# Two extra tokens as zero columns in a Strassen product: 512 columns in one bank for three products of seven

## The chip, the core and the metric

The kernel runs on one core of a Trainium2 chip. The core has five engines that run side by side and meet through semaphores: TensorE (PE, matrix products into PSUM), VectorE (DVE), ScalarE (ACT), GpSimd (POOL) and SyncE (SP, which here only issues transfers). PSUM has eight banks of 512 float32 values per partition; one matmul writes one bank.

The metric is the device time of one execution in microseconds (us), lower is better; the median of the runs is compared.

## The reference

One layer of a decoder trunk on 1,024 tokens of width 1,024, with 16 learned meta tokens ahead of them:

```python
u = rmsnorm(h, mix_norm_pre[l])
proj = u @ w_in[l]
q, f_logit, i_in, g_out, v_pool, gate_a, gate_b = jnp.split(proj, cuts, axis=-1)
a = hgrn2(q, f_logit, i_in, g_out, lbs[l], hgrn_out_norm[l])
p = multiscale_pool(v_pool, pool_proj[l], pool_scale[l])
z = (jax.nn.sigmoid(gate_a) * (a @ w_branch_hgrn[l])
     + jax.nn.sigmoid(gate_b) * (p @ w_branch_pool[l]))
h = h + rmsnorm(z @ w_out[l], mix_norm_post[l])
u = rmsnorm(h, ffn_norm_pre[l])
gt = causal_dwconv(u @ ffn_w_gate[l], ffn_conv_w[l], ffn_conv_b[l])
y = (jax.nn.gelu(gt, approximate=True) * (u @ ffn_w_up[l])) @ ffn_w_down[l]
h = h + rmsnorm(y, ffn_norm_post[l])
return h[:, N_META:]
```

`gate_a` and `gate_b` are 1,024 wide each, the MLP's gate and up 2,816. The convolution `causal_dwconv` looks at a token and the two before it. Because of it the MLP's gate needs two tokens ahead of the 1,024 that are returned: 1,026 in all (`TQ`), which the kernel also uses for the mixer's gates.

## The kernel before

Float32 accuracy comes from splitting every operand into a high and a low part in the fast float32 format (`hi`, `lo`) and forming three matmuls: hi x hi, hi x lo, lo x hi. Weights are the stationary operand, tokens the moving one.

**Strassen.** The mixer's two gates and the MLP's gate and up are formed with Strassen's scheme in Winograd's form (`class Strassen`): the weight block of 256 output features ("unit") is cut in four, the tokens' activations too (features in two halves of 512, tokens in two halves), and seven products P1 to P7 take the place of eight. The seven stream these quarters or sums of them (`MOVING`): P1 b11, P2 b21, P3 b22, P4 t4, P5 t1, P6 t2, P7 t3, where t1 = b12 - b11, t2 = b22 - t1, t3 = b22 - b12 and t4 = b21 - t2. The order is P1 P2 P6 P5 P3 P7 P4. Sums of the products give the four output blocks: C11 = P1 + P2, and with U2 = P1 + P6 and U3 = U2 + P7, C12 = U2 + P5 + P3, C22 = U3 + P5 and C21 = U3 + P4 (signs are folded into the sums of weights). DVE forms them, reading the products from PSUM (`rest`, `put`).

Each quarter is 4 blocks of 128 features, so a product is 4 x 3 matmuls for each group of columns. There are 8 units in the mixer's gates, 11 gate units and 11 up units in the MLP.

**The halves of the tokens.** `HT` is 514 and `HALO` 2. For a gate the first half is tokens 0 to 513, the second 512 to 1025: the two overlap by two tokens, and both are 514 wide. A product of 514 columns doesn't fit in a bank, so `product` cuts it into 258 + 256 columns, in the two banks of a pair (offset 254), 24 matmuls a product. The up units need no extra tokens: their span skips the first two columns and has 512, 12 matmuls a product in one bank.

**Where the quarters lie.** In the mixer b11, b21 and b22 are read from the tiles of u (`uhi`, `ulo`, a row of 1,040 values for each block of features); t1 to t4 lie in slots of 4,160 bytes a partition, two blocks of features in each. In the MLP b11 and b21 lie in a tile v1, b22 and t1 in v2, with 514 values a block, and t2, t3, t4 in slots. Slots come from one pool of 24 and are reused by the pool's own order.

**The sums of the activations.** In the mixer `gate_steps(d)` forms t1 to t4 for one group of tokens d: four groups of 128 and one of the two first tokens (`ds[0]`). `SUMS_AT` says by hand at which point of the first stage each step is issued; the order of ACT, DVE and PE is written out there (`manual_schedule`). `put` writes a high part on ACT and a low part on the engine given.

In the MLP the rows of the residual come in nine row tiles of 114 tokens (`RT`), in three thirds of three. While PE forms z @ w_out for one third (8 steps of k), the rows of the third before are normed, transposed by PE into a spare pair of PSUM banks (`feat`, `to_quarters`, L1172) and put into the quarters: the first half's tokens into b11 and b21, the second half's into b22 and the sums. Row tile 4 holds the border between the halves. PE has four pairs of banks there: three hold the third's own products, one takes the transposes. In the last third `add_quarters` opens the slots of t2, t3, t4 at k = 3.

**What the products feed.** `put_gate` adds the products, takes the sigmoid on ACT and stores the gate to a scratch tensor, from which the mixer's end loads it. `put_ffn` writes the gate into a tile of 2 x 514 values (`gate_tile`); `conv` reads that in three shifted views of 2 x 512 on DVE, ACT applies gelu, and the up unit's sums are multiplied in (`whole_ffn`, `store_y`). Then the down product runs as a Strassen scheme of its own, with both operands in one tile (`rot`, rows of 2,048 bytes for each operand half); the last part of it reads operands that were prepared early and held in slots.

Most orders in the MLP's products and after are left to a scheduler, except POOL's, written out by hand.

Of the kernel before, what the change touches and what calls it, by code (L numbers as in the profile page):

```python
# [32 lines left out]
LUP = 2.0 ** 60  # L33
KT = 6
HT = 514
EARLY = 4
EARLY_G = 2
SUMS_AT = {5: (2,), 6: (2, 1), 8: (3,), 9: (1, 3), 10: (1, 4), 11: (4, 0), 12: (0, 0)}
# [18 lines left out]
def trunk_kernel(ctx: ExitStack, tc: tile.TileContext, x, meta_tokens, mix_norm_pre,  # L57
# [132 lines left out]
    class Strassen:  # L190
# [7 lines left out]
        def __init__(self, units, run, early, quarters, span, put, whole):  # L198
            self.units, self.run, self.early, self.bq = units, run, early, quarters
            self.span, self.put, self.whole = span, put, whole  # L200
# [65 lines left out]
        def product(self, u, p, onto=None):  # L266

            assert self.seq[self.at] == (u, p)
            x = pair(p) if onto is None else onto
            self.at += 1  # L270
            whi, wlo = self.got[self.at - 1]
            q = self.MOVING[p]
            c0, o0, n = self.span(u)
            cuts = [(c0, o0, 512 - o0), (c0 + 512 - o0, 512, n - 512 + o0)][: 1 + (n + o0 > 512)]
            go = dict(skip_group_check=onto is not None)
            for k in range(4):
                xh, xl = (self.bq[q + h][k * len(self.bq[q + h]) // 4] for h in "hl")
                kk = k % xh.shape[1]
                xh, xl = xh[:, kk, :], xl[:, kk, :]
                for c, o, w in cuts:  # L280
                    d = x[:, o : o + w]
                    pe.matmul(d, whi[:, k, :], xh[:, c : c + w], start=(k == 0 and onto is None), stop=False, **go)  # L282
                    pe.matmul(d, whi[:, k, :], xl[:, c : c + w], start=False, stop=False, **go)  # L283
                for c, o, w in cuts:
                    pe.matmul(x[:, o : o + w], wlo[:, k, :], xh[:, c : c + w], start=False, stop=(k == 3), **go)  # L285
            self.ahead(self.lead)
            return x if onto is not None else (x if self.whole_pair else x[:, o0 : o0 + n])

        lead, whole_pair = 4, False

        def half(self, key, i, n, name):

# [24 lines left out]
        def rest(self, u, between=None):  # L317

            def then(p):
                for f in (between or {}).get(p, ()):  # L320
                    f()

            u2 = self.p1s[u]
            dve.tensor_tensor(u2, u2, self.product(u, "P6"), ALU.add)
            then("P6")
            x5 = self.product(u, "P5")
            then("P5")
            self.put(u, 0, 1, u2, x5, self.product(u, "P3"))
# [507 lines left out]

    def load_gate(d, b, m):
        d[m] = slot(TQ, name="sa")
# [94 lines left out]
    order = ORDER.split()  # L933
    order = [(o_[:-1], int(o_[-1])) for o_ in order]
    gq = {}
    for q, i, t0 in (("b11", 0, T0), ("b21", 1, T0), ("b22", 1, T0 + 512)):
        for h, u in (("h", uhi), ("l", ulo)):
            gq[q + h] = [u[:, 4 * i : 4 * i + 4, t0 : t0 + HT]]

    def two_halves(q):  # L940
        for h in "hl":
            gq[q + h] = [slot(2 * HT, F32R, q + h).rearrange("p (k t) -> p k t", k=2) for _ in range(2)]

    def gate_steps(d):
        a, b = (slice(T0 + d.start + o, T0 + d.stop + o) for o in (0, 512))
        (b11h, b11l), (b21h, b21l), (b12h, b12l), (b22h, b22l) = (
            [rr(u[:, 4 * i : 4 * i + 4, c]) for u in (uhi, ulo)] for i, c in ((0, a), (1, a), (0, b), (1, b)))
        if a.start in t12:
            t1, t2 = t12[a.start]
        else:  # L950
            t1, t2 = halves_tmp(d.stop - d.start)
            dve.tensor_tensor(t2, b12l, b11l, ALU.subtract)
            dve.tensor_tensor(t1, b12h, b11h, ALU.subtract)
            dve.tensor_tensor(t1, t1, t2, ALU.add)
            dve.tensor_tensor(t2, b22h, t1, ALU.subtract)
# [7 lines left out]
        dve.tensor_tensor(t2, t2, b21l, ALU.add)  # L963
# [6 lines left out]
    gates = Strassen([(WIN, c + 2 * P * j) for c in (CA, CB) for j in range(KD // 2)], range(KD), EARLY, gq,  # L970
                     lambda u: (0, 254, HT), put_gate, lambda u, i: None)

    vb = [bank("pv") for _ in range(2)]
    E = mybir.EngineType
    with tc.manual_schedule(engines={E.Activation, E.DVE, E.PE}):
# [34 lines left out]
        for i in range(2, len(vtiles)):  # L1010
# [10 lines left out]
                params()  # L1021
            if i == 5:
                for q in ("t2", "t1", "t3", "t4"):
                    two_halves(q)
# [95 lines left out]
    for t, names in ((v1, ("b11h", "b11l", "b21h", "b21l")), (v2, ("b22h", "b22l", "t1h", "t1l"))):  # L1120
        for i, n in enumerate(names):
            fq[n] = [t[:, i * Q : (i + 1) * Q].rearrange("p (k t) -> p k t", k=4)]
# [44 lines left out]
    def to_quarters(un, t_at, banks, eng):  # L1167
# [26 lines left out]

        def difference():
            dve.tensor_tensor(c12, c22, c12, ALU.subtract)
            put("t3", c12, d, dve)

        return [first_sums, lambda: put("t1", t1, d, dve), lambda: put("b22", c22, d, eng), difference,
                lambda: negdiff(eng, t2, t2, "b21", d), lambda: put("t4", t2, d, eng)]  # L1200

    def combine(eng, dst, src, op, q, d):
# [102 lines left out]
    def span(up):  # L1305
        return (2, 0, HT - 2) if up else (0, 254, HT)

    gs, ya_ = {}, {}

    def gate_tile(m):  # L1310
        if m not in gs:
            gs[m] = slot(2 * HT, name="g").rearrange("p (h t) -> p h t", h=2)
        return gs[m]

    def conv(m):
        if m not in ya_:
            ya_[m] = slot(SEQ, name="y").rearrange("p (h t) -> p h t", h=2)
        g, a = gs[m], ya_[m]
        n = HT - HALO
        dve.tensor_scalar(a, g[:, :, 2 : 2 + n], cvw[:, 2, m : m + 1], cvb[:, m : m + 1], ALU.mult, ALU.add)  # L1320
        for j in (1, 0):
            dve.scalar_tensor_tensor(a, g[:, :, j : j + n], cvw[:, j, m : m + 1], a, ALU.mult, ALU.add)  # L1322
        act.activation(a, a, AF.Gelu_apprx_tanh)

    def put_ffn(u, i, h, a, b, c=None):

        j, up = UNITS[u]
        m = 2 * j + i
        d = ffn.half(("u", u), 1, HT - HALO, "w") if up else gate_tile(m)[:, h]
# [8 lines left out]
    def whole_ffn(u, i):  # L1338
# [12 lines left out]
        if u == len(UNITS) - 1 and i == 0:  # L1351
            preps[0] = prep(0, 0)

    ffn = Strassen([((ffn_w_up if up else ffn_w_gate)[0], 2 * j * P) for j, up in UNITS], RUN, EARLY, fq,
                   lambda u: span(UNITS[u][1]), put_ffn, whole_ffn)


    big, loads, preps, rot = [], {}, {}, [0]
# [51 lines left out]
    with tc.manual_schedule(engines={E.PE, E.Activation, E.DVE, E.Pool}):  # L1410
# [57 lines left out]

        def second(e):
            ffn.product(e, "P2", x[e])  # L1470
            act.copy(gate_tile(2 * UNITS[e][0])[:, 0], x[e][:, o : o + n])

        def do(i, n=1):
            for _ in range(n):
# [182 lines left out]
```

## Time and profile before

| | |
|---|---|
| median of 3 runs | 1370.23 us (1370.08 to 1371.32) |
| span of the profiled execution, first to last instruction | 1366.5 us |
| mean granted TensorE clock | 0.998 |
| HBM traffic over the span | 189 GB/s |

By stage, as the profile's order of time shows it: input norm, values and two output gates to 90 us; the mixer's gates by Strassen to 250; the recurrence, pooling and branches to about 600; z @ w_out to 705; the MLP's gate and up products to 1145; the down product and the last norm to the end.

How to read the lines below: a row of a group or of the order of time has the start and duration in us (in stretches: the window, its length), the engine, the source line, the operation, the tiles written and read, and the shapes; [x <- y] is idle time of that engine just before and what ended it. PE's matmuls are pipelined, so a row's duration is longer than the distance to the next start. "PEld" is the load of the stationary operand, which overlaps.

### The profile page before, as it was taken

The numbers are of one execution on the slowest core, as the hardware profiler recorded it, in microseconds if no ns is written. First come the engines' busy times: TensorE is split into PE (matmuls) and PEld (weight loads), VectorE is DVE, ScalarE is ACT, GpSimd is POOL, SyncE is SP. The second block draws the span as 40 slices with busy tenths as digits, with TensorE's granted clock in tenths as the row PEclk, the third lists the DMA queues.
The fourth block names the chain that finished last, engine by engine and source line by source line (L and its number), as shares of the span: only waits on it lengthen the run. The fifth ranks groups of instructions, "written<-read, shape, count | busy, mean of one in ns | idle before, by whom it ended". The sixth has DMA issues, their size and how long they took to land. (4 is left out here: it accounts for less than half of the span.)

```text
span 1366.5 us, 21661 instructions
## 1 busy us (share of the span) xinstructions
PE 1343.0 (98%) x8421; PEld 1216.9 (89%) x8421; DVE 956.5 (70%) x1421; ACT 565.6 (41%) x942; POOL 440.7 (32%) x326
## 2 busy tenths in 40 slices
PE   8999999999999999999999999999999999999997
PEld 7799999999999899987788888988899997888786
DVE  6764645388886768766568888878878776744557
ACT  5543333367455474225654222222222223543343
POOL 2015421237544600051021555354556742000100
PEclk9999999999999999999999999999999999999999
DMA  7134333311110148989876777766676789965514
GB/s 265 44 118 142 117 116 105 104 49 45 34 50 18 34 147 294 320 286 310 298 285 222 212 200 201 200 178 165 160 180 152 176 238 265 380 216 188 185 62 169
DMA packets 141460, 236.76 MB, mean 173 GB/s; under 512 B 9254, under 2 KB 77450, under 8 KB 141358
## 3 DMA queue, kind: packets, MB, share of 16 engines
q1 hardware_dynamic: 129294, 211.00, 45.5%
q0 software_dynamic: 12064, 24.38, 10.3%
q8 instruction: 66, 1.08, 0.3%
q14 instruction: 36, 0.29, 0.1%
HBM read 171.85 MB, written 86.53 MB: 189 GB/s over the span
## 5 line engine op out<-in xcount | busy, mean ns | idle before, releaser
L282 PE MATMUL P<-v,whi 128*128 128x258 f32 (+1 forms) x496 | 153.2, 323 | 2.3 <-ACT p L1463 1.7
L283 PE MATMUL P<-v,whi 128*128 128x258 f32 (+1 forms) x496 | 152.5, 321 | 0.0
L285 PE MATMUL P<-v,wlo 128*128 128x256 f32 (+2 forms) x512 | 136.5, 320 | 0.0
L171 PE MATMUL pd<-rot 128*128 128x512 f32 x272 | 106.0, 390 | 0.3 <-DVE rot L1390 0.3
L172 PE MATMUL pd<-rot 128*128 128x512 f32 x272 | 105.8, 389 | 0.0
L282 PEld LDWEIGHTS P<-v,whi 128*128 128x128 f32 x496 | 93.4, 188 | 10.7 <-ACT p L1463 2.1
L283 PEld LDWEIGHTS P<-v,whi 128*128 128x128 f32 x496 | 93.7, 189 | 7.5
L137 POOL TENSOR_TENSOR wlo<-wraw,whi 128x1024 fp32r<-128x1024 f32 (+1 forms) x19 | 45.8, 2413 | 167.7 <-ACT whi L136 97.5
L285 PEld LDWEIGHTS P<-v,wlo 128*128 128x128 f32 x512 | 84.8, 188 | 7.6
L1390 DVE TENSOR_TENSOR rot<-yt,rot 128x1024 fp32r<-128x1024 f32 x33 | 41.2, 1250 | 71.7 <-ACT rot L1389 71.6
L227 ACT CAST whi<-wraw 128x512 fp32r<-128x512 f32 x78 | 46.0, 617 | 99.3 <-PE P L283 88.5
L228 DVE TENSOR_TENSOR wlo<-wraw,whi 128x512 fp32r<-128x512 f32 x74 | 68.1, 942 | 19.9 <-ACT whi L227 19.9
L1274 POOL TENSOR_TENSOR ys<-y 128x512 f32<-128x512 f32 x22 | 35.9, 1630 | 139.4 <-issue 94.9
L170 PE MATMUL pd<-rot 128*128 128x512 f32 x272 | 72.9, 391 | 2.1 <-ACT rot L1389 1.2
L253 POOL TENSOR_TENSOR swa<-wraw,wraw 128x512 f32<-128x512 f32 x28 | 43.3, 1546 | 94.6 <-DMA wraw<-in_w_in_dram 61.5
L1389 ACT CAST rot<-yt 128x1024 fp32r<-128x1024 f32 x33 | 34.6, 1052 | 90.3 <-PE pd L171 90.3
L227 ACT CAST whi<-swa 128x512 fp32r<-128x512 f32 x56 | 33.3, 618 | 89.8 <-PE P L283 77.4
L136 ACT CAST whi<-wraw 128x1024 fp32r<-128x1024 f32 (+1 forms) x28 | 26.4, 942 | 102.0 <-PE ppv L184 21.2
L1322 DVE SCALAR_TENSOR_TENSOR y<-g,par,y 128x1024 f32<-128x1024 f32 x44 | 66.5, 1512 | 0.8
L170 PEld LDWEIGHTS pd<-rot 128*128 128x128 f32 x272 | 50.8, 188 | 14.0 <-ACT rot L1389 2.3
L171 PEld LDWEIGHTS pd<-rot 128*128 128x128 f32 x272 | 51.0, 188 | 11.3 <-DVE rot L1390 0.7
L172 PEld LDWEIGHTS pd<-rot 128*128 128x128 f32 x272 | 51.1, 188 | 10.7
(375 smaller groups left out, 4276.0 us busy)
## 6 DMA issues: line engine op xcount, KB each, us to landing
wraw<-in_w_in_dram SPq DMA_DIRECT2D x36, 512.0 KB
yt<-ysum SPq DMA_DIRECT2D x33, 512.0 KB
wraw<-in_ffn_w_gate_dram SPq DMA_DIRECT2D x26, 512.0 KB
wraw<-in_w_out_dram SPq DMA_DIRECT2D x24, 512.0 KB
wraw<-in_ffn_w_up_dram SPq DMA_DIRECT2D x22, 512.0 KB
wsum<-in_ffn_w_down_dram SPq DMA_DIRECT2D x22, 512.0 KB
ysum<-ys SPq DMA_DIRECT2D x11, 768.0 KB
sa<-sscr SPq DMA_DIRECT2D x16, 513.0 KB
```

Source lines behind the costliest of these rows:

```text
L137: eng.tensor_tensor(lo, raw, rr(hi), ALU.subtract)
L170: pe.matmul(ps, ahi, bhi, start=first, stop=False)
L171: pe.matmul(ps, ahi, blo, start=False, stop=False)
L172: pe.matmul(ps, alo, bhi, start=False, stop=last)
L227: act.copy(hi, src)
L228: (pool_e if 4 <= i < 2 * self.early else dve).tensor_tensor(lo, src, rr(hi), ALU.subtract)
L253: pool_e.tensor_tensor(s1, a21, a22, ALU.add)
L282: pe.matmul(d, whi[:, k, :], xh[:, c : c + w], start=(k == 0 and onto is None), stop=False, **go)
L283: pe.matmul(d, whi[:, k, :], xl[:, c : c + w], start=False, stop=False, **go)
L285: pe.matmul(x[:, o : o + w], wlo[:, k, :], xh[:, c : c + w], start=False, stop=(k == 3), **go)
L1322: dve.scalar_tensor_tensor(a, g[:, :, j : j + n], cvw[:, j, m : m + 1], a, ALU.mult, ALU.add)
L1390: dve.tensor_tensor(lo, src, rr(hi), ALU.subtract)
```

## The change

The two halves no longer overlap. The first half keeps 514 tokens (0 to 513); the second half is the 512 tokens 514 to 1025. For the first two tokens the second half has no partner: they meet columns of zeros. With b12 = b22 = 0 there, t1 is -b11, t2 is b11, t3 is 0 and t4 is b21 - b11. P3 and P7 are zero for those columns, and P5 only enters blocks of the second half, where they aren't wanted. So P3, P5 and P7 (`SECOND`) stream 512 columns from the first column of b22, t1 and t3, in one bank; P1, P2, P6 and P4 of a gate unit stay at 514 (258 + 256), and those of an up unit skip the first two columns as before. The sums take `own`, the last 512 columns of U2, where P3, P5 or P7 comes in.

The two tokens' values of t2 (a copy) and t4 (three operations and a split) come from a new function `halo_sums`. In the mixer it takes the place of the three steps of `ds[0]`, as one step; in the MLP it is called in `add_quarters`.

Storage: b22 and t1 of the MLP have 512 values a block in v2, t1 and t3 have slots of 2 x 512, t2 and t4 stay at 2 x 514. The gate tile is one row of 1,026, and the convolution reads 1,024 contiguous values.

```diff
+HN = HT - HALO
...
+        SECOND = ("P3", "P5", "P7")
...
-            c0, o0, n = self.span(u)
+            c0, o0, n = self.span(u, p)
...
+        def span(self, u, p="P1"):
+
+            if p in self.SECOND:
+                return 0, 0, HN
+            return (0, 512 - HN // 2 - HALO, HT) if self.halo(u) else (HALO, 0, HN)
+
+        def own(self, u, t):
+            return t[:, HALO:] if self.halo(u) else t
...
-            self.put(u, 0, 1, u2, x5, self.product(u, "P3"))
+            own = self.own(u, u2)
+            self.put(u, 0, 1, own, x5, self.product(u, "P3"))
             then("P3")
             self.whole(u, 0)
-            dve.tensor_tensor(u2, u2, self.product(u, "P7"), ALU.add)
-            self.put(u, 1, 1, u2, x5)
+            dve.tensor_tensor(own, own, self.product(u, "P7"), ALU.add)
+            self.put(u, 1, 1, own, x5)
             self.put(u, 1, 0, u2, self.product(u, "P4"))
...
     def put_gate(u, i, h, a, b, c=None):
-        g = slot(HT, name="sg")
+        at = slice(HT, TQ) if h else slice(0, HT)
+        g = slot(at.stop - at.start, name="sg")
...
-        if h == 0:
-            nc.sync.dma_start(sd[2 * u + i, :, :HT], g)
-        else:
-            nc.sync.dma_start(sd[2 * u + i, :, HT:], g[:, HALO:])
+        nc.sync.dma_start(sd[2 * u + i, :, at], g)
...
+    def halo_sums(bq, d):
+
+        for h in "hl":
+            for ks, t in parts("t2" + h, d, bq):
+                act.copy(t, rr(bq["b11" + h][0][:, ks, d]))
+        t4 = small([P, 4 * HALO], "t4", "t4", 2).rearrange("p (k t) -> p k t", k=4)
+        dve.tensor_tensor(t4, rr(bq["b21h"][0][:, :, d]), rr(bq["b11h"][0][:, :, d]), ALU.subtract)
+        dve.tensor_tensor(t4, t4, rr(bq["b11l"][0][:, :, d]), ALU.subtract)
+        dve.tensor_tensor(t4, t4, rr(bq["b21l"][0][:, :, d]), ALU.add)
+        put("t4", t4, d, dve, bq)
+
     def gate_steps(d):
+        if d.start == 0:
+            halo_sums(gq, d)
+            yield
+            return
+        s_ = slice(d.start - HALO, d.stop - HALO)
...
-        put("t1", t1, d, dve, gq)
+        put("t1", t1, s_, dve, gq)
...
-        put("t3", t1, d, dve, gq)
+        put("t3", t1, s_, dve, gq)
...
-    Q = 4 * HT
-    v1, v2 = ubig(F32R, "v1", 4 * Q), ubig(F32R, "v2", 4 * Q)
...
+    for n, name, names in ((HT, "v1", ("b11h", "b11l", "b21h", "b21l")), (HN, "v2", ("b22h", "b22l", "t1h", "t1l"))):
+        t = ubig(F32R, name, 16 * n)
+        for i, q in enumerate(names):
+            fq[q] = [t[:, i * 4 * n : (i + 1) * 4 * n].rearrange("p (k t) -> p k t", k=4)]
 
     def add_quarters(*names):
         for q in names:
-            for h in "hl":
-                fq[q + h] = [slot(2 * HT, F32R, q + h).rearrange("p (k t) -> p k t", k=2) for _ in range(2)]
+            two_halves(fq, q)
+        halo_sums(fq, slice(0, HALO))
...
-        f = max(0, HT - HALO - t_at)
+        f = max(0, HT - t_at)
         n2 = RT - f
...
-        d = slice(t_at + f - (HT - HALO), t_at + RT - (HT - HALO))
+        s_ = slice(t_at + f - HT, t_at + RT - HT)
+        d = slice(s_.start + HALO, s_.stop + HALO)
...
-            gs[m] = slot(2 * HT, name="g").rearrange("p (h t) -> p h t", h=2)
+            gs[m] = slot(TQ, name="g")
...
-        g, a = gs[m], ya_[m]
-        n = HT - HALO
-        dve.tensor_scalar(a, g[:, :, 2 : 2 + n], cvw[:, 2, m : m + 1], cvb[:, m : m + 1], ALU.mult, ALU.add)
+        g, a = gs[m], ya_[m].rearrange("p h t -> p (h t)")
+        dve.tensor_scalar(a, g[:, 2 : 2 + SEQ], cvw[:, 2, m : m + 1], cvb[:, m : m + 1], ALU.mult, ALU.add)
```

More of the change, by code (lines that the diff above doesn't have):

```diff
@@ L196, in trunk_kernel, with __init__ @@
         MOVING = dict(P1="b11", P2="b21", P3="b22", P4="t4", P5="t1", P6="t2", P7="t3")
-        def __init__(self, units, run, early, quarters, span, put, whole):
+        SECOND = ("P3", "P5", "P7")
+        def __init__(self, units, run, early, quarters, halo, put, whole):
             self.units, self.run, self.early, self.bq = units, run, early, quarters
-            self.span, self.put, self.whole = span, put, whole
+            self.halo, self.put, self.whole = halo, put, whole
             self.raws, self.sums, self.p1s, self.halves = {}, {}, {}, {}
@@ L935, in trunk_kernel, with two_halves @@
     gq = {}
-    for q, i, t0 in (("b11", 0, T0), ("b21", 1, T0), ("b22", 1, T0 + 512)):
+    for q, i, t0, n in (("b11", 0, T0, HT), ("b21", 1, T0, HT), ("b22", 1, T0 + HT, HN)):
         for h, u in (("h", uhi), ("l", ulo)):
-            gq[q + h] = [u[:, 4 * i : 4 * i + 4, t0 : t0 + HT]]
-    def two_halves(q):
+            gq[q + h] = [u[:, 4 * i : 4 * i + 4, t0 : t0 + n]]
+    def two_halves(dst, q):
+        n = HN if q in ("t1", "t3") else HT
         for h in "hl":
-            gq[q + h] = [slot(2 * HT, F32R, q + h).rearrange("p (k t) -> p k t", k=2) for _ in range(2)]
-    def gate_steps(d):
+            dst[q + h] = [slot(2 * n, F32R, q + h).rearrange("p (k t) -> p k t", k=2) for _ in range(2)]
+    def halo_sums(bq, d):
[7 more added lines that the diff above has]
+        put("t4", t4, d, dve, bq)
+    def gate_steps(d):
+        if d.start == 0:
[3 more added lines that the diff above has]
+        s_ = slice(d.start - HALO, d.stop - HALO)
         a, b = (slice(T0 + d.start + o, T0 + d.stop + o) for o in (0, 512))
@@ L970, in trunk_kernel @@
     gates = Strassen([(WIN, c + 2 * P * j) for c in (CA, CB) for j in range(KD // 2)], range(KD), EARLY, gq,
-                     lambda u: (0, 254, HT), put_gate, lambda u, i: None)
+                     lambda u: True, put_gate, lambda u, i: None)
     vb = [bank("pv") for _ in range(2)]
@@ L1023, in trunk_kernel @@
                 for q in ("t2", "t1", "t3", "t4"):
-                    two_halves(q)
+                    two_halves(gq, q)
                 sums = [gate_steps(d) for d in ds]
@@ L1114, in trunk_kernel @@
     open_pool("pf", 4, PSUM)
-    Q = 4 * HT
-    v1, v2 = ubig(F32R, "v1", 4 * Q), ubig(F32R, "v2", 4 * Q)
     fq = {}
-    for t, names in ((v1, ("b11h", "b11l", "b21h", "b21l")), (v2, ("b22h", "b22l", "t1h", "t1l"))):
-        for i, n in enumerate(names):
-            fq[n] = [t[:, i * Q : (i + 1) * Q].rearrange("p (k t) -> p k t", k=4)]
+    for n, name, names in ((HT, "v1", ("b11h", "b11l", "b21h", "b21l")), (HN, "v2", ("b22h", "b22l", "t1h", "t1l"))):
+        t = ubig(F32R, name, 16 * n)
+        for i, q in enumerate(names):
+            fq[q] = [t[:, i * 4 * n : (i + 1) * 4 * n].rearrange("p (k t) -> p k t", k=4)]
     def add_quarters(*names):
         for q in names:
-            for h in "hl":
-                fq[q + h] = [slot(2 * HT, F32R, q + h).rearrange("p (k t) -> p k t", k=2) for _ in range(2)]
+            two_halves(fq, q)
+        halo_sums(fq, slice(0, HALO))
     g2 = gain_bc(mix_norm_post, "g2")
@@ L1196, in difference @@
             dve.tensor_tensor(c12, c22, c12, ALU.subtract)
-            put("t3", c12, d, dve)
-        return [first_sums, lambda: put("t1", t1, d, dve), lambda: put("b22", c22, d, eng), difference,
+            put("t3", c12, s_, dve)
+        return [first_sums, lambda: put("t1", t1, s_, dve), lambda: put("b22", c22, s_, eng), difference,
                 lambda: negdiff(eng, t2, t2, "b21", d), lambda: put("t4", t2, d, eng)]
@@ L1303, in trunk_kernel @@
     RUN = [u for e in range(EARLY) for u in (e, e + EARLY)] + list(range(2 * EARLY, len(UNITS)))
-    def span(up):
-        return (2, 0, HT - 2) if up else (0, 254, HT)
     gs, ya_ = {}, {}
@@ L1317, in conv @@
             ya_[m] = slot(SEQ, name="y").rearrange("p (h t) -> p h t", h=2)
[L1318 to L1320 removed]
+        g, a = gs[m], ya_[m].rearrange("p h t -> p (h t)")
+        dve.tensor_scalar(a, g[:, 2 : 2 + SEQ], cvw[:, 2, m : m + 1], cvb[:, m : m + 1], ALU.mult, ALU.add)
         for j in (1, 0):
[L1322 removed]
+            dve.scalar_tensor_tensor(a, g[:, j : j + SEQ], cvw[:, j, m : m + 1], a, ALU.mult, ALU.add)
         act.activation(a, a, AF.Gelu_apprx_tanh)
@@ L1328, in put_ffn @@
         m = 2 * j + i
-        d = ffn.half(("u", u), 1, HT - HALO, "w") if up else gate_tile(m)[:, h]
+        d = ffn.half(("u", u), 1, HN, "w") if up else gate_tile(m)[:, slice(HT, TQ) if h else slice(0, HT)]
         dve.tensor_tensor(d, a, b, ALU.add)
@@ L1354, in trunk_kernel @@
     ffn = Strassen([((ffn_w_up if up else ffn_w_gate)[0], 2 * j * P) for j, up in UNITS], RUN, EARLY, fq,
-                   lambda u: span(UNITS[u][1]), put_ffn, whole_ffn)
+                   lambda u: not UNITS[u][1], put_ffn, whole_ffn)
     big, loads, preps, rot = [], {}, {}, [0]
@@ L1470, in second @@
             ffn.product(e, "P2", x[e])
-            act.copy(gate_tile(2 * UNITS[e][0])[:, 0], x[e][:, o : o + n])
+            act.copy(gate_tile(2 * UNITS[e][0])[:, :HT], x[e][:, o : o + n])
         def do(i, n=1):
```

## The prediction

> **What bounds the kernel now.** I read the page's busy times first, then the stretches by stage, then stretches that hold one kind of matmul alone, then the order of time around the one place where the change adds work in front of TensorE.
>
> ```profile
> span 1366.5 us, 21661 instructions
> PE 1343.0 (98%) x8421; PEld 1216.9 (89%) x8421; DVE 956.5 (70%) x1421; ACT 565.6 (41%) x942; POOL 440.7 (32%) x326
> ```
>
> A busy share counts overlapping matmuls, so 98% alone says little; what counts is whether TensorE (PE) ever waits in the stages that the change touches.
>
> ```profile
> core 0: us, PE busy (x) PEld busy (x) DVE busy (x) ACT busy (x) POOL busy (x), PEclk, DMA share, GB/s
> 90.00:250.00 160.00, 159.76 (x1341) 159.49 (x1341) 76.70 (x115) 56.46 (x104) 55.24 (x38) 1.00 0.35 117
> ...
> 660.00:700.00 40.00, 38.82 (x181) 29.35 (x180) 24.50 (x42) 24.22 (x51) 2.92 (x4) 1.00 0.80 281
> ...
> 760.00:1120.00 360.00, 360.00 (x2273) 325.42 (x2273) 294.42 (x351) 99.45 (x162) 206.69 (x153) 1.00 0.70 182
> ```
>
> The gates' products of the mixer (90 to 250 us) and the products of the MLP (from about 700 us; the row takes 760 to 1120) leave PE 0.24 us and 0.00 us idle, at a granted clock of 1.00. There a nanosecond less per matmul is a nanosecond less of the span. Between them, at 660 to 700 us, PE idles 1.18 us.
>
> What one matmul costs is the distance from start to start, not the duration in a row (an instruction of 512 columns is shown as 390 ns and followed after about 230). I take it from stretches cut at starts; the count in brackets includes one or two instructions that lap over an edge, so I divide by the count of the code.
>
> ```profile
> core 0: us, PE busy (x), PEclk, DMA share, GB/s
> 90.53:250.60 160.07, 160.07 (x1345) 1.00 0.35 118
> 888.82:908.30 19.48, 19.48 (x86) 1.00 0.52 160
> 908.30:928.38 20.08, 20.08 (x170) 1.00 0.74 185
> 1207.55:1261.95 54.40, 54.40 (x241) 1.00 0.59 195
> 1342.70:1355.85 13.15, 13.15 (x58) 1.00 0.55 208
> ```
>
> - Mixer gates: 8 units x 7 products x 24 = 1344 matmuls of 258 or 256 columns: 160.07 / 1344 = 119.1 ns, so 238.2 ns for a pair.
> - One MLP gate unit: 7 x 24 = 168 such matmuls: 20.08 / 168 = 119.5 ns, a pair 239.0 ns.
> - One up unit, 7 x 12 = 84 matmuls of 512 columns: 19.48 / 84 = 231.9 ns. These already run the way the change wants.
> - The down product, 240 matmuls of 512 columns: 54.40 / 240 = 226.7 ns. Both its operands lie in one tile with rows of 2,048 bytes.
> - The last down products, whose operands lie in separate slots of 4,160 bytes, in the same stage: 13.15 / 57 = 230.7 ns.
>
> **The merged matmuls.** P3, P5 and P7 of a gate unit each lose 12 of 24 matmuls: 4 blocks of k x 3 matmuls, each a pair of 258 + 256 columns that becomes one of 512. That is 36 pairs a unit, 8 x 36 = 288 in the mixer and 11 x 36 = 396 in the MLP; 684 in all, which is also the difference between the two built programs' PE rows (7626 and 6942). With the up unit's 231.9 ns for the single matmul: 288 x (238.2 - 231.9) = 1.8 us and 396 x (239.0 - 231.9) = 2.8 us, together **-4.6 us**. Both stretches are PE-dense by the rows above, so all of it reaches the end. The bounds are the down stage's 226.7 ns (684 x 5.2 = 3.6 us more) and the slope alone, 684 x 2 columns x 0.45 ns = 0.6 us, if only columns cost time.
>
> A page of the Trainium skill, "TensorE: Matmul & The Clock Gate", section "Back-to-back issue gap", gives the isolated gap of a warm matmul as columns / 2.4 + 2.5 ns. By that a pair would be 219.2 ns and the single one 215.8, the saving 3.3 ns or 684 x 3.3 = 2.3 us, an estimate from the page. The trace disagrees on both: 239.0 and 231.9 ns.
>
> **The layout of b22 and t1.** v2 held rows of 514 columns; now b22 and t1 of the MLP are 512 wide and lie in it at 2,048 bytes a row, like the down product's tile. P3 and P5 of all 22 units, the up units too, stream them: 22 x 2 x 12 = 528 matmuls. The two bounds are 231.9 ns (nothing) and 226.7 ns (528 x 5.2 = 2.7 us less). I take 226.7, because the two rows of the down stage differ in layout and hardly in anything else: same width, same stage, 226.7 ns in one tile and 230.7 ns in slots. **-2.7 us.** t3 and the mixer's t1 stay in slots and the mixer's b22 stays in the tile of u, whose rows are 4,160 bytes, so P7 and the mixer's three products get the 231.9 of the sum above; at 226.7 their 420 would give 2.2 us more, which goes into the range.
>
> **The extra tokens' own sums.** In the mixer they replace a chain of 25 small instructions by 11 and move before G1's sigmoids.
>
> ```profile
> start us, us, engine line op out<-in xcount [idle before <-releaser]
> 87.12 0.71 ACT L357 CAST t4h<-tt 128x256 fp32r<-128x256 f32 x2 [0.62 <-DVE tt L963]
> 90.02 1.15 ACT L770 ACTIVATE sg<-pg 128x342 f32<-128x342 f32 x3 [2.18 <-PE pg L187]
> 91.05 0.30 ACT L357 CAST t1h<-tt 128x4 fp32r<-128x4 f32 x2
> 91.22 0.31 ACT L357 CAST t2h<-tt 128x4 fp32r<-128x4 f32 x2
> ...
> 88.57 0.17 DVE L954 TENSOR_TENSOR tt<-tt 128x8 f32<-128x8 f32 x1
> 88.77 0.17 DVE L955 TENSOR_TENSOR tt<-uhi,tt 128x8 f32<-128x8 f32 x1
> ```
>
> ACT idles 2.18 us there, until PE ends G1. Three DVE operations at 0.20 us and six ACT ones at 0.085 (two pairs start 0.17 apart) end near 89.3, before 90.02: **0**. Were that cover gone, the sigmoids would be up to 1.5 us late and the first gate product with them.
>
> In the MLP the extra tokens had no instructions of their own: they rode in the blocks of the row tiles. Now eleven new ones are issued once, when the last third's fourth k-step is queued: four ACT copies into t2, three DVE operations and a two-part split for t4. In the new order ACT has the six between the copy of zc (L1070) and the cast of v from PSUM (L357), DVE its three behind the subtraction of zc (L1071).
>
> ```profile
> start us, us, engine line op out<-in xcount [idle before <-releaser]
> 687.25 1.05 ACT L1145 CAST whi<-wraw 128x1024 fp32r<-128x1024 f32 x1 [3.93 <-DMA wraw<-in_w_out_dram]
> 688.21 0.47 ACT L1070 CAST zc<-sa 128x342 fp32r<-128x342 f32 x1
> 688.58 0.35 ACT L357 CAST v<-pt 128x232 fp32r<-128x232 f32 x1
> ...
> 690.64 0.36 ACT L1188 COPY tt<-pt 128x232 f32<-128x232 f32 x1
> ...
> 688.71 0.52 DVE L1071 TENSOR_TENSOR zc<-sa,zc 128x342 fp32r<-128x342 f32 x1 [4.73 <-ACT zc L1070]
> 689.14 0.39 DVE L358 TENSOR_TENSOR v<-pt,v 128x232 fp32r<-128x232 f32 x1
> ...
> 691.05 1.00 PE L1172 MATMUL pt<-ident,un 114*128 114x114 f32 x8 [0.85 <-ACT tt L1188]
> ```
>
> This lies on PE's path: at 691.05 PE has waited 0.85 us for ACT's copy of 690.64, which frees the only spare PSUM pair, and everything queued behind it waits too. With the change: DVE starts t4 at 689.14, three steps of 0.20 end near 689.7, ACT's two casts of t4 end near 690.0, and only then comes the cast of v that stood at 688.58. DVE's part of v, which ACT's later copies wait for, moves from 689.14 to about 690.4. So PE's wait grows by about **+1.3 us**. The bounds are 0 (w_out's load, for which ACT sat 3.93 us, lands earlier) and 2.0 (every hand-over pays another 0.1).
>
> **Edits at nothing.** Sums on DVE and ACT lose 2 of 514 columns, row tile 4 loses 2 of 58, and one store of y now stands behind two loads on SP's queue near 1140 us, its reader being the last down pass. The convolution reads one row of 1,024 in place of 2 x 512, the same elements; it costs something only if DVE, idle 65.58 us of the 360 in the row above, runs out of slack, about 1 us on each of its 66 instructions (3 for each of 22 blocks). The store and loads of the gates keep their bytes.
>
> **The sum.** -4.6 - 2.7 + 1.3 = -6.0 us. The profiled execution has a span of 1366.5, so 1360.5 after; the median of the runs, 1370.23, lies 3.7 above the span, and with the same 3.7 the time is **1364.2 us**.
>
> **Rivals.**
> - *The layout brings nothing* (231.9 for all): -4.6 + 1.3, 1366.9. For it: the down stage is another stage, with other traffic. Against: its last products, in slots, are back at 230.7.
> - *The halo's wait is hidden*: 1362.9. For it: ACT's 3.93 us of idling just before; against: that wait is for a load queued behind stores that follow PE's own work, so it moves along.
> - *Columns are what costs*: a saving of 0.6 us, +1.3, 1370.9, no change. Against: 231.9 and 239.0 ns stand side by side in one stage. By the 2.3 us of the Trainium skill's page "TensorE: Matmul & The Clock Gate" (section "Back-to-back issue gap") it would be 1369.2.
> - *The gain is waited away at a join*: PE meets a transfer that doesn't move with it, 1369 to 1371. For it: DMA at 0.80 in 660 to 700 us. Against: PE idles only 1.18 us there, and the loads are issued when PE's own readers free a buffer.
>
> The last rival needs the first writes of now to the slots of t2 and t4, the stores of the residual rows, and SP's waits for these stores (in total, times, longest):
>
> ```profile
> 692.15 0.48 ACT L357 CAST t2h<-tt 128x116 fp32r<-128x116 f32 x2 [1.15 <-DVE tt L1192]
> ...
> 702.80 0.46 ACT L357 CAST t4h<-tt 128x116 fp32r<-128x116 f32 x2
> ...
> 672.11 0.68 SPq L1246 DMA_DIRECT2D hscr<-m  x2
> ...
> 673.50 1.59 SPq L1246 DMA_DIRECT2D hscr<-m  x2
> ...
> SPq L1161 <- DMA hscr<-m: 2.4, 3, 0.9
> ```
>
> - *Slower: the early halo waits for its slots.* The first writes to the slots of t2 and t4 come 3 to 13 us earlier than now, and in the built program one ACT copy and one DVE split wait for stores of the residual rows that used the slots before. ACT then stands, with the cast of v, the copies of 690.64 and PE behind it. The stores go out at 672 to 675 us; PE is no later than now while they land before about 695 (688.7 plus the 6.0 saved), beyond that each microsecond is lost. At 700 us the time would be 1375. Against it is the longest wait for these stores on SP, 0.9 us.
>
> **How the numbers follow.** Forecast 0.46, no layout gain 0.22, halo hidden 0.10, columns only 0.04, waited away 0.08, slower 0.10. A change under 0.2% (2.7 us) can't be told from none. Faster than that are the forecast, the hidden halo and most of the layout rival, 0.72; same 0.18; slower 0.10. The range reaches down to the slots' bound (1364.2 - 2.2 = 1362.0, a little less with a part of the halo hidden) and up past the layout rival with a halo of 2.0 (1367.6): 1361.5 to 1368.0.
>
> **What would show it.** Gate units of 168 matmuls become 132. By my numbers one takes 48 pairs at 239.0 = 11.5 us, 24 matmuls at 226.7 = 5.4 us and 12 at 231.9 = 2.8 us: 19.7 us, and an up unit 19.4. If both keep 231.9 for P3 and P5, the layout step is wrong. At the mixer's end PE should be 1.8 us earlier. PE's wait before the transposes that follow the fourth k-step of the last third should be near 2.2 us in place of 0.85; if it is 0.85 or less, the halo step is wrong, and if it is over 8 the slower case holds. PE idle inside 760 to 1120 us would show that another engine has become the bound.

## The result and the profile after

The changed kernel takes 1365.14 us (median of 5 runs, 1363.17 to 1367.33); the kernel before, run beside it, 1371.32 us (median of 5, 1370.08 to 1373.98). The ratio is 0.9954, with a 95% interval of 0.9941 to 0.9967: 0.3 to 0.6% faster. The forecast was 1364.2 us, in a range of 1361.5 to 1368.0.

The page of the changed kernel, its span and its busy times:

```profile
span 1361.5 us, 20285 instructions
...
PE 1336.0 (98%) x7737; PEld 1181.8 (87%) x7737; DVE 952.4 (70%) x1414; ACT 565.9 (42%) x946; POOL 439.2 (32%) x326
```

684 matmuls less, and a span 5.0 us shorter than the 1366.5 of before. To see where they went I cut both executions at the same instructions: where a stage's first matmul starts, and around the stall in front of the transposes. First the stretches of before, then those of after (window, length, PE busy and matmuls, granted clock, DMA share, GB/s; the first stretch of before, the mixer's gates, is 160.07 us in the prediction):

```profile
451.39:500.76 49.37, 46.88 (x310) 0.97 0.19 59
500.76:689.80 189.04, 186.93 (x1014) 1.00 0.89 303
689.80:732.41 42.61, 39.73 (x280) 1.00 0.65 230
732.41:1146.70 414.29, 412.79 (x2583) 1.00 0.73 194
```

```profile
90.42:248.83 158.41, 158.41 (x1057) 1.00 0.37 118
449.57:497.38 47.81, 45.34 (x310) 1.00 0.20 63
497.38:687.96 190.58, 187.16 (x1014) 1.00 0.90 301
687.96:731.98 44.02, 40.78 (x279) 0.96 0.62 219
731.98:1141.87 409.89, 408.14 (x2188) 1.00 0.74 196
```

| stretch | before | after | difference |
|---|---|---|---|
| mixer's gates | 160.07 | 158.41 | -1.66 |
| pooling, untouched by the change | 49.37 | 47.81 | -1.56 |
| branches and z @ w_out, up to the last matmul ahead of the stall | 189.04 | 190.58 | +1.54 |
| stall, rest of z @ w_out, first products of the MLP | 42.61 | 44.02 | +1.41 |
| rest of the MLP's products | 414.29 | 409.89 | -4.40 |

The five add up to -4.67; the remaining 0.3 us of the 5.0 are spread over the start and the end. Two rows weren't forecast, and they cancel. The pooling stage holds a wait of PE for ACT of 2.5 us in both kernels, but of these two profiles only that of before has the clock lowered after it: 0.97 against 1.00 over the stretch. It is a matter of the profiled execution and not of the change: seven of the twelve profiles of changed kernels (e1, e2, e3, e6, e9, e10, e11) have 49.1 to 49.4 us here too. In the next stretch, where the DMA engines are at 0.9, PE has a new wait:

```profile
PE ppv L184 <- ACT st L735: 2.5, 1, 2.5
PE pt L1198 <- ACT tt L1215: 2.0, 1, 2.0
...
PE pm L172 <- DMA wlo<-wlos: 1.4, 1, 1.4
PE P L284 <- ACT p L1486: 1.2, 1, 1.2
```

These are PE's waits after the change (line waited at, releaser; in total, times, longest). No wait for wlo stands in the same list of before. That PE came 3.4 us early to this stretch (497.38 in place of 500.76) doesn't explain it: e5 below, the same kernel coming as early, takes 4 us longer here, and e1, whose PE came 3.4 us later than before, waits for wlo just as long, 1.4 us. The stretch in e5 and in e1:

```profile
497.22:691.80 194.58, 188.97 (x1015) 0.99 0.89 296
504.19:696.34 192.15, 187.43 (x1014) 1.00 0.90 298
```

In the twelve profiles of changed kernels it goes from 189.95 to 194.58 us, with waits for wlo of 1.0 to 3.4 in each; of before there is one profile, 189.04 without such a wait. So this stretch alone scatters by over 4 us between profiles, and whether the change has a part in the +1.54 is open.

The stretches of one MLP gate unit, one up unit, and the twelve matmuls of P3 in that up unit, after and then before (the units of before are in the prediction):

```profile
905.96:925.66 19.70, 19.70 (x134) 1.00 0.77 192
925.66:945.11 19.45, 19.45 (x87) 1.00 0.48 140
936.83:939.55 2.72, 2.72 (x14) 1.00 0.89 212
```

```profile
939.52:942.29 2.77, 2.77 (x13) 1.00 0.67 96
```

The gate unit is at 19.70 us as forecast, the up unit at 19.45 where 19.36 follows from the forecast's terms. P3 is at 2.72 / 12 = 226.7 ns a matmul, from 230.8.

The order of time after the change, at the place where the prediction set the eleven new instructions:

```profile
685.41 1.05 ACT L1171 CAST whi<-wraw 128x1024 fp32r<-128x1024 f32 x1 [4.16 <-DMA wraw<-in_w_out_dram]
686.37 0.47 ACT L1097 CAST zc<-sa 128x342 fp32r<-128x342 f32 x1
686.74 0.29 ACT L959 CAST t2h<-v 128x4 fp32r<-128x4 f32 x2
...
687.90 0.29 ACT L369 CAST t4h<-t 128x4 fp32r<-128x4 f32 x2 [0.68 <-DVE t L963]
688.10 0.34 ACT L369 CAST v<-pt 128x232 fp32r<-128x232 f32 x1
...
689.96 0.35 ACT L1215 COPY tt<-pt 128x224 f32<-128x224 f32 x1
```

```profile
690.37 1.00 PE L1198 MATMUL pt<-ident,un 114*128 114x114 f32 x8 [2.01 <-ACT tt L1215]
```

The cast of v stands 1.73 us behind that of zc (686.37 to 688.10) where it stood 0.37 behind it; ACT waits 0.68 us in between for the three steps on DVE. PE's wait is 2.01 us instead of 0.85. No DMA is named as releaser of t2h or t4h.

### The profile page after: what moved, and what is told of

Read it like the earlier page. It is cut to its first block, busy times and chain, and to the rows that moved or that the text cites. A ratio compares the mean times of both kernels' runs of the same rounds, so it can differ in the third digit from the quotient of the medians.

```text
span 1361.5 us, 20285 instructions
## 1 busy us (share of the span) xinstructions
PE 1336.0 (98%) x7737; PEld 1181.8 (87%) x7737; DVE 952.4 (70%) x1414; ACT 565.9 (42%) x946; POOL 439.2 (32%) x326
## 5 line engine op out<-in xcount | busy, mean ns | idle before, releaser
L284 PE MATMUL P<-v,whi 128*128 128x512 f32 (+2 forms) x408 | 141.5, 354 | 2.1 <-ACT p L1486 1.2
L285 PE MATMUL P<-v,whi 128*128 128x512 f32 (+2 forms) x408 | 141.0, 353 | 0.0
L287 PE MATMUL P<-v,wlo 128*128 128x512 f32 (+2 forms) x424 | 135.6, 350 | 0.0
L284 PEld LDWEIGHTS P<-v,whi 128*128 128x128 f32 x408 | 76.8, 188 | 13.1 <-ACT p L1486 1.4
L285 PEld LDWEIGHTS P<-v,whi 128*128 128x128 f32 x408 | 76.9, 189 | 10.6
L287 PEld LDWEIGHTS P<-v,wlo 128*128 128x128 f32 x424 | 74.2, 188 | 11.0
L171 PEld LDWEIGHTS pd<-rot 128*128 128x128 f32 x272 | 50.9, 188 | 13.7 <-ACT rot L1412 2.0
L229 ACT CAST whi<-swb 128x512 fp32r<-128x512 f32 x56 | 33.4, 619 | 67.2 <-PE P L285 63.1
L172 PEld LDWEIGHTS pd<-rot 128*128 128x128 f32 x272 | 51.1, 188 | 11.3 <-DVE rot L1413 0.7
```

What stands on the lines that cost most here:

```text
L171: pe.matmul(ps, ahi, bhi, start=first, stop=False)
L172: pe.matmul(ps, ahi, blo, start=False, stop=False)
L229: act.copy(hi, src)
```

## The experiments

All but e5 are edits of the changed kernel.

**e1: the extra tokens' sums earlier.** `add_quarters` is issued ahead of the step's loads and of zc:

```diff
+                if c == 2 and k == 3:
+                    add_quarters("t2", "t3", "t4")
...
-                        if c == 2 and k == 3:
-                            add_quarters("t2", "t3", "t4")
```

> The extra tokens' sums are issued ahead of the last step's loads and of zc, while ACT waits 4.16 us for whi (its row at 685.41 after the change). Theory (the sums delay ACT's cast of v, that delays the copy which frees PE's PSUM pair, and PE's wait of 2.01 us is what the half-clock stretch of 691 to 694.5 us follows): PE's wait before the transposes at about 690 us falls from 2.01 to about 0.85 us, that stretch runs at a granted clock of 1.00, and the span falls by 1.2 + 1.5 = 2.7 us, to about 1358.8; at least by 1.2, to 1360.3, if the half clock turns up at another wait. Rival 1 (the first writes to the slots of t2 and t4 wait for stores of residual rows): ACT or DVE shows a DMA as the releaser of t2h or t4h, PE's wait stays at 2 us or grows, span 1361.5 or more. Rival 2 (the gain is given back at the next join): the wait is gone at 690 us and comes back as a wait for wlo or whi before 705 us, span within 0.5 us of 1361.5.

Measured: 1364.73 us (median of 5, 1362.09 to 1370.49), ratio to before 0.9940 (0.9926 to 0.9953). The profiled execution was the longest of the five, 1368.8 us of span: PE waited 3.7 us for DVE in the recurrence, in instructions that the edit doesn't touch. So the span says nothing here; the stretch around the stall does, cut at the same two instructions as above (e1's PE row, its waits, its stretch):

```profile
697.56 1.00 PE L1198 MATMUL pt<-ident,un 114*128 114x114 f32 x8 [0.82 <-ACT tt L1215]
```

```profile
PE sl L649 <- DVE d L634: 3.7, 1, 3.7
...
PE P L284 <- ACT p L1486: 1.8, 2, 1.2
```

```profile
696.34:739.16 42.82, 39.87 (x279) 1.00 0.63 226
```

The wait is back at 0.82 us, and the stretch takes 42.82 us where the change took 44.02 and before 42.61. Rival 1, waiting for slots, is refuted. The 1.2 us arrive, the further 1.5 for the clock don't: PE waits twice instead of once for the copies of L1486.

**e2: rows of 514 values again**, read 512 wide:

```diff
-        t = ubig(F32R, name, 16 * n)
+        t = ubig(F32R, name, 16 * HT)
...
-            fq[q] = [t[:, i * 4 * n : (i + 1) * 4 * n].rearrange("p (k t) -> p k t", k=4)]
+            fq[q] = [t[:, i * 4 * HT : (i + 1) * 4 * HT].rearrange("p (k t) -> p k t", k=4)[:, :, :n]]
```

> The MLP's b22 and t1 lie at rows of 514 values (2,056 bytes) again and are still read 512 wide: the layout alone is undone. Theory (a matmul's distance depends on the rows of what it streams): P3 and P5 of the MLP's units go from 226.7 to 230.1 ns back to about 231.9 ns each; a gate unit grows from 19.69 by 12 x 5.2 + 12 x 3.5 ns to 19.80 us, an up unit from 19.45 by 12 x 5.2 + 12 x 1.8 ns to 19.53 us, together 11 x 0.19 = 2.1 us of span; 1.3 us if the P1 and P2 of up units, which became 2.0 and 3.5 ns slower with the change, turn back too. Rival (the gain came from the 512 columns or from the merge itself): P3 stays at 226.7 ns, a gate unit at 19.69 and an up unit at 19.45 us.

Measured: 1369.9 us in one run. The stretches of the up unit, the gate unit and the up unit's P3:

```profile
931.37:950.92 19.55, 19.55 (x86) 1.00 0.48 141
911.55:931.37 19.82, 19.82 (x133) 1.00 0.77 189
942.58:945.36 2.78, 2.78 (x13) 1.00 0.89 220
```

P3 goes back to 2.78 / 12 = 231.7 ns, a gate unit is 0.12 us longer and an up unit 0.10: 11 x 0.22 = 2.4 us. The theory holds, the rival falls. With the same merge as the change but without its layout, this kernel also shows what the merge alone did: a gate unit 20.08 - 19.82 = 0.26 us shorter than before, 11 x 0.26 = 2.9 us, and an up unit 0.07 us longer.

**e3: the products cut again**, over two banks, with the columns left at 512:

```diff
             if p in self.SECOND:
-                return 0, 0, HN
+                return 0, 256 if self.halo(u) else 0, HN
```

> P3, P5 and P7 of the gates are cut into 256 + 256 columns over two banks again: the merge alone is undone, 684 matmuls more, the columns stay 512. Theory (each matmul costs something for being one): a pair takes 238.2 to 239.0 ns less 0.9 ns for two columns, so about 237.7, against 231.9 of the mixer's single one; mixer 288 x 5.8 = 1.7 us longer; MLP 132 pairs of P7 x 5.8 = 0.8 us, 264 pairs of P3 and P5 x 10 = 2.6 us if the halves do not keep the gain of the rows, x 5.8 = 1.5 us if they do: span 4.0 to 5.1 us longer, a gate unit 19.69 + 0.2 to 0.3 us. Rival (only columns cost): nothing, a gate unit stays at 19.69 us and the mixer's products within 0.2 us.

Measured: 1372.54 us in one run. The mixer's gates, then an MLP gate unit and an up unit:

```profile
90.58:250.15 159.57, 159.57 (x1345) 1.00 0.36 118
913.57:933.64 20.07, 20.07 (x170) 1.00 0.76 191
933.64:953.01 19.37, 19.37 (x86) 1.00 0.54 156
```

The mixer is 1.16 us longer than with the change, so 1.16 / 288 = 4.0 ns for each pair in place of a single matmul; the other 0.50 us of the mixer's gain are the two columns and what comes with them. A gate unit is 0.37 us longer, more than the 0.2 to 0.3 expected: the halves of 256 columns do not keep the gain of the rows. By these rows undoing the merge costs 1.16 + 11 x 0.37 - 11 x 0.08 = 4.4 us; the span is 9.3 us longer, and most of the rest lies in stages that the edit doesn't touch (pooling 1.5, branches and z @ w_out 2.8). The rival that only columns cost is refuted in both stages. By the Trainium skill's page "TensorE: Matmul & The Clock Gate", section "Back-to-back issue gap", the constant of the isolated gap of a warm matmul is 2.5 ns; the 4.0 measured here is larger.

**e4: the extra tokens' sums twice.**

```diff
-        halo_sums(fq, slice(0, HALO))
+        for _ in range(2):
+            halo_sums(fq, slice(0, HALO))
```

> The extra tokens' sums of the MLP are issued twice in a row at their place; the second time writes the same values. Theory (they lie on ACT's and DVE's path to the copy that frees PE's PSUM pair): PE's wait before the transposes at about 690 us grows from 2.01 by about as much as the first set cost, 1.16 us, to 3.2 us, and the half clock after it is there again: span 1361.5 + 1.2. Rival (the wait of 2.01 us comes from the load of w_out, which lands when it lands, and the sums are hidden behind it): the wait stays at 2.0 us.

Measured: 1364.18 us in one run, span 1362.5. PE's row and the stretch:

```profile
691.49 1.78 PE L1199 MATMUL pt<-ident,un 114*128 114x114 f32 x8 [3.06 <-ACT tt L1216]
```

```profile
688.03:733.00 44.97, 40.71 (x280) 0.96 0.60 214
```

The second set costs 1.05 us of wait and 0.95 us of the stretch, and the span is 1.0 us longer. The sums lie on the path at nearly full price; the rival, a wait for w_out's load, is refuted.

**e5 and e6: the changed kernel and the early sums, on one chip.** No new edits.

> The changed kernel as it is, on the same chip and in the same rounds as the next run. Theory (half clock after PE's wait of 2.0 us comes in some executions only: it followed in the change's profile and in that of the doubled sums, and not in those of the 514 rows and of the cut products, each with a wait of 1.98 to 2.02 us): the wait is 2.0 us again, the MLP's gate unit 19.69 and the up unit 19.45 us, and the times lie around 1365 with a spread of 3 to 4 us from lowest to highest. Rival (the half clock belongs to the kernel): it is there again at 691 us, at a granted clock near 0.54.

> The early sums once more, beside the changed kernel on one chip. Theory (the wait of 2.0 us is 0.8 here, and what is won reaches the end less what the copies of L1486 on ACT take back at the first MLP products, where PE waited 0.78 + 1.39 us in the first run of it and 1.39 in the change's profile): 1.2 us less wait, at most 0.8 of it given back, so the median lies 0.4 to 1.2 us under that of the change; with a half clock avoided, up to 2.5. Rival (all of it is given back): the medians agree within 0.3 us or its own is higher.

Measured: the changed kernel 1365.79 us (median of 12, 1363.30 to 1375.56), ratio to before 0.9968 (0.9953 to 0.9983); the early sums 1364.64 us (median of 6, 1362.09 to 1367.01), ratio 0.9958 (0.9945 to 0.9972). The stretch of e5, then that of e6:

```profile
691.80:735.82 44.02, 40.80 (x279) 0.96 0.61 216
```

```profile
691.98:734.85 42.87, 39.88 (x280) 1.00 0.65 233
```

In both profiles of each kernel the stretch is the same within 0.05 us: 44.02 and 44.02, 42.82 and 42.87. So 1.2 us is what the early place is worth, and the medians differ by as much (1.15 us, within the 0.4 to 1.2 expected). The changed kernel's times spread over 12.3 us and not the 3 to 4 expected; without the longest it is 4.4. The intervals overlap; the times alone don't settle that e6 is faster than the change, the profiles do for this stretch.

**The clock after the stall.** e5's theory was that a lowered clock follows the 2.0 us wait in some executions only, and e1's that it costs 1.5 us. PE's row at the stall and the stretch without it, in e2:

```profile
694.73 1.00 PE L1198 MATMUL pt<-ident,un 114*128 114x114 f32 x8 [2.02 <-ACT tt L1215]
```

```profile
692.31:736.43 44.12, 39.96 (x279) 1.00 0.61 217
```

PE waited 2.02 us here too, the granted clock stayed at 1.00, and the stretch is no shorter than the change's 44.02 at 0.96. The PE busy time is 0.82 us less and comes back as idle time: PE arrives earlier at the first MLP products and waits for ACT's copies of L1486, 1.8 us in two waits where the change has one of 1.2. In the nine profiles with a wait of 1.98 to 2.07 us the stretch takes 44.00 to 44.12 us, five times with the lowered clock and four times without. So e1's price of 1.5 us was wrong: at this place the lowered clock is covered by ACT. In e5's own profile the half clock was there again, as its rival had it; for its theory speak e2, e3, e7 and e9, in which PE does the same work around the wait and the clock stays at 1.00.

**e7 to e11: where the rows of b22 and t1 start.** All keep 2,048 bytes from row to row. In e7 the low parts lie 8 bytes further than the high parts, in e8 to e11 the whole tile lies 8, 16, 32 or 64 bytes further than in the change, where rows start 256 bytes past a multiple of 2,048. The edit of e8, in e9 to e11 with another shift (e7 shifts b22's low part and t1's high part by 8 bytes, t1's low part by 16):

```diff
-        t = ubig(F32R, name, 16 * n)
+        t = ubig(F32R, name, 16 * n + 8)
...
-            fq[q] = [t[:, i * 4 * n : (i + 1) * 4 * n].rearrange("p (k t) -> p k t", k=4)]
+            at = i * 4 * n + 2 * (n == HN)
+            fq[q] = [t[:, at : at + 4 * n].rearrange("p (k t) -> p k t", k=4)]
```

> In the MLP's tile of b22 and t1 the low parts lie 8 bytes further than the high parts, all rows still 2,048 bytes apart. Theory A (a matmul is at 226.7 ns when its rows start at the same place within 2,048 bytes as those of the matmul before it): high and low alternate, so P3 goes back to about 231.9 ns, P5 to 233, a gate unit to 19.82 us. Theory B (the distance of the rows alone, or their start at a multiple of 8 bytes, decides): P3 stays at 226.7 ns, the unit at 19.69.

> The whole tile of the MLP's b22 and t1 lies 8 bytes further, high and low parts alike, rows 2,048 bytes apart. Theory A (only that all rows start at the same place within 2,048 bytes): P3 stays at 226.7 ns, a gate unit at 19.69 us. Theory C (that each row starts at a multiple of a larger block than 8 bytes): P3 goes back to about 231.9 ns, the unit to 19.82 us. If both shifted kernels keep 226.7 ns, the distance of the rows alone decides; if both lose it, theory C.

> All rows of the MLP's b22 and t1 lie 16 bytes further. In the shift of 8 bytes every matmul of P3 took 233.3 ns, without any variation, in place of 226.7; the rows of the changed kernel start at 256 bytes past a multiple of 2,048. Theory (a row that starts inside a block of the memory costs one more block to read; the 6.6 ns are near 16 columns = 64 bytes, of 226.7 ns x 16 / 512 = 7.1): 233.3 ns again. Rival (the block is 16 bytes or less): 226.7 ns.

> All rows of the MLP's b22 and t1 lie 32 bytes further. Theory (blocks of 64 bytes): P3 at 233.3 ns. Rival (blocks of 32 bytes): 226.7 ns.

> All rows of the MLP's b22 and t1 lie 64 bytes further, at 320 bytes past a multiple of 2,048. Theory (blocks of 64 bytes): P3 at 226.7 ns, a gate unit at 19.69 us. Rival (larger blocks, up to 256 bytes): 233.3 ns, a gate unit at 19.85 us. After PE's wait of about 2.0 us near 690 us the half clock comes in some of these three runs and not in others, if it belongs to the execution; if it belongs to the kernel, in all three.

Measured, one run each: 1368.32, 1365.47, 1367.93, 1370.49 and 1367.86 us, which scatter by more than the effect. P3 of one up unit in e7, e8, e9, e10 and e11, in this order:

```profile
940.09:942.90 2.81, 2.81 (x13) 1.00 0.87 211
```

```profile
937.86:940.66 2.80, 2.80 (x14) 1.00 0.94 203
```

```profile
940.79:943.57 2.78, 2.78 (x14) 1.00 0.86 216
```

```profile
942.91:945.71 2.80, 2.80 (x13) 1.00 0.92 204
```

```profile
941.34:944.09 2.75, 2.75 (x14) 1.00 0.87 137
```

| rows of P3 | ns a matmul (length / 12) |
|---|---|
| as changed | 226.7 |
| low parts 8 bytes further | 234.2 |
| all 8 bytes further | 233.3 |
| all 16 bytes further | 231.7 |
| all 32 bytes further | 233.3 |
| all 64 bytes further | 229.2 |
| 514 values a row (e2) | 231.7 |

The same rows at the same distance lose the whole gain when they start 8 bytes later. So theory B (the distance decides) and theory A (equal starts decide) are refuted. Blocks of 64 bytes, which e10 agrees with, asked for 233.3 in e9, where it is 231.7, and for 226.7 in e11; larger blocks asked for 233.3 there; it is 229.2, between them. That the start of the rows matters is shown, as nothing else that PE reads or writes differs in these kernels; the rule by which it does is open.

## Why the prediction was right, and where it was not

- **The merge**, -1.8 and -2.8: right. The mixer's gates gained 1.66 us, the MLP's gate units 2.9 (e2 against before), and e3 shows that most of the mixer's part is the second instruction and not the columns.
- **The layout**, -2.7: right, e2 loses 2.4 without it, and the rival that it brings nothing falls. The reason given was too simple: rows of 2,048 bytes are not enough, e8 has them and is at 233.3 ns.
- **The up units** are the step that was mis-sized. The prediction left all of an up unit but P3 and P5 as it was, 19.48 - 24 x 5.2 ns = 19.36 us. It is 19.45, 11 x 0.09 = 1.0 us over the eleven. P5 has only a part of the gain, and P1 and P2, which the change doesn't touch, take 5.60 us in place of 5.54 for their 24 matmuls. The rows, before and after:

```profile
928.38:933.92 5.54, 5.54 (x27) 1.00 0.02 5
```

```profile
925.66:931.26 5.60, 5.60 (x26) 1.00 0.01 5
```

  In e1, e3 and e6 they are at 5.54 or 5.55, in the other experiments at 5.61, with the same tile of v1 at the same place. e9 has both, an early and a later up unit:

```profile
783.91:789.52 5.61, 5.61 (x26) 1.00 0.43 60
929.69:935.23 5.54, 5.54 (x27) 1.00 0.02 5
```

  So with the same rows of v1 in one execution the two products take either time: what they stream and where it lies doesn't decide it alone. What does isn't settled.
- **The sums in the mixer**, 0: nothing contradicts it, the mixer's gates run without a gap.
- **The sums in the MLP**, +1.3: right. The wait grew by 1.16 us, the stretch by 1.41, doubling cost 0.95 and the earlier place saved 1.2. The rivals that the sums are hidden and that they wait for slots are refuted, by e4 and by the rows of t2h and t4h.
- **Waited away at a join**, a rival with 0.08, may have happened in part: the stretch before the stall is 1.54 us longer and has a new wait for wlo of 1.4. But it takes 190.58 and 194.58 us in two executions of the same changed kernel, so one profile of before can't show that the change costs anything there.
- The forecast span of 1360.5 was 1361.5. The three terms gave -1.66 - 4.40 + 1.41 = -4.65 instead of -6.0; the pooling stage (-1.56) and the join (+1.54) cancelled. The first of them belongs to the clock of the profiled execution of before and not to the change. That the time came within 1 us of the forecast was in part luck, also because the prediction took the 3.7 us from the span to the median as fixed: each of the recorded runs is 1.7 to 1.8 us above its own span, and the rest is that both profiled executions were some 2 us faster than the median.

## What to carry to other kernels

Where PE never idles, an instruction saved is worth its fixed cost at every repetition (4.0 ns here), and where the streamed rows start can be worth as much (226.7 to 234.2 ns for the same 512 columns): measure start-to-start distances per product, not the time of the whole. A handful of tiny instructions costs 1.2 us when they are queued ahead of the copy that frees PE's only spare buffer, and next to nothing some instructions earlier (42.82 us of stretch against 42.61 before): place them where their engine waits for a load. To price a local edit in executions that scatter by 4 us, cut both profiles at the same two instructions around it: the stretch around the stall repeated within 0.1 us while the times did not. A stretch in which PE waits for loads doesn't repeat like that (190.58 and 194.58 us of one kernel).

## What was not expected of the hardware

A wait of PE of about 2 us lowers the granted clock afterwards in some profiles and not in others, though PE does the same work around it. Of ten profiles with a wait of 1.98 us or more at this place six show it (the change, e4, e5, e8, e10, e11) and four don't (e2, e3, e7, e9); the three with 0.82 to 0.86 us (before, e1, e6) don't.

What goes with it in all ten is where the wait falls in a fixed grid of time. Each of these lowered stretches lasts 3.41 us, and where one profile has several, their starts are whole multiples of 3.413 us apart: 653.30 and 694.26 us in e5 (12), 463.18, 650.91 and 695.28 in e10 (55 and 13). Laid from a profile's lowered stretches over its wait, the grid gives these two windows for the change (the one with the wait, the next), and these for e2, whose nearest lowered stretch starts 67 windows earlier, at 464.88 us (length, PE busy and matmuls, granted clock, DMA share, GB/s):

```profile
687.92:691.33 3.41, 1.40 (x11) 1.00 0.87 334
691.33:694.74 3.41, 3.41 (x10) 0.50 0.19 79
```

```profile
690.15:693.57 3.42, 2.56 (x12) 1.00 1.02 411
693.57:696.98 3.41, 2.25 (x15) 1.00 0.64 238
```

In the change one window holds the whole wait, 2.01 us idle, and the next runs at half clock. In e2 an edge cuts the wait into 0.86 and 1.16, and the clock stays. So it is in all ten: in the six with the lowered clock 1.94 to 2.81 us of idle time lie in one window, in the four without at most 1.59. At other places the idle time of a window doesn't sort them as cleanly: e6 is lowered at 563.32 us after 1.57 us idle, e11 isn't at 651.53 after 1.83.

The page "TensorE: Matmul & The Clock Gate" of the Trainium skill, section "What's actually happening", describes a free-running window of 3,413 ns on the activity of PE, and the traces agree with 3.413 us; its section "Why this matters for your kernels" warns of gaps over about 3 us only, and here 2.0 us were enough.
